# Row skewness on one core: wider loads at the start, part of the row sums on ACT, and the last two blocks closed together

## The chip, the cores and the metric

The kernel runs on one core of one Trainium2 chip. The metric is the device time of one execution in microseconds (us); lower is better. Engines are named as in the profile: PE (TensorE), DVE (VectorE), ACT (ScalarE), POOL (GpSimd), SP (SyncE, which issues the transfers here).

## The reference

The input `x` is 1024 x 8192 in float32 (33.55 MB). For each row the skewness is wanted:

```python
mean = np.mean(x, axis=-1, keepdims=True)
std = np.std(x, axis=-1, keepdims=True)
z = (x - mean) / (std + 1e-8)
return np.mean(z ** 3, axis=-1)
```

Both kernels compute it from three sums of each row: m1 = sum(x)/n, m2 = sum(x^2)/n, m3 = sum(x^3)/n. With var = m2 - m1^2 the result is (m3 - 3 m1 (var + m1^2/3)) * var^-1.5.

## The kernel before, in words

The 1024 rows are 8 blocks of 128 rows, one row a partition. A block's 8192 columns are loaded in units, whose widths stand in `UNITS`, one list a block. A unit is named (block, number), both from 0: (6,2) is the third unit of block 6. The loop at L118 goes over the blocks, the loop at L123 over the units of one. SP issues one load a unit (L125) into one of `X_BUFS` = 8 buffers, so a load waits until the unit eight places earlier has been read by all.

Each unit is cut in equal pieces of at most 2304 columns (`_slices`). For a piece:

- ACT squares it, scaled so that the sum is m2's share, into `sq` (four buffers), and adds up along the row (`accum_out`, L135). A second, short instruction reads the accumulator.
- DVE multiplies `sq` by `x` and adds up along the row (L139): the third sums. This instruction is called a cube below.

PE adds up the columns of a block: it transposes each 128 x 128 piece of `x` against the identity, accumulating all 64 of a block in one PSUM tile `tp` (L145). When the block is through, ACT copies `tp` to `tsb` (L115) and a matmul with a column of 1/8192 gives m1 in one column of `s1ps` (L116).

Each piece's second and third sum has a column of its own in `s2u` and `s3u`; block 7 has its own tiles `s2l` and `s3l`. When block 6 is through, `finish_first_blocks` closes blocks 0 to 6 together: two reduces on DVE (L97), three operations on ACT (L101 to L103), six on POOL (L106 to L111), the power var^-1.5 among them. Block 7 is closed at the end: its m2 by an accumulating copy on ACT (L156), its m3 by a reduce on DVE (L157), m1 squared, variance and the bracket on ACT (L160, L161, L164, L165), the power on POOL (L163), and the numerator on DVE (L166) and the product (L169). Then PE transposes the 128 x 8 results (L172), DVE copies them from PSUM (L174), and SP writes them out (L175).

In the last two units of block 7 the squares go to PSUM (`psq`) and the cubes to a small tile `cubes`, instead of both to the same SBUF buffer.

A scheduler that works from the order of the program sets the order of the instructions on each engine; an instruction whose operands are late can be passed by a later one.

Of the kernel before, what the change touches and what calls it, by code (L numbers as in the profile page):

```python
# [8 lines left out]
FP = mybir.dt.float32  # L9
AF = mybir.ActivationFunctionType  # L10
ALU = mybir.AluOpType
X_AXIS = mybir.AxisListType.X


UNITS = [
    [512, 1024, 2560, 4096],
    [4096, 4096],
    [4096, 4096],
    [4352, 3840],
    [3328, 2816, 2048],  # L20
    [2048, 2048, 2048, 2048],
    [1792, 1792, 1664, 1536, 1408],
    [1152, 1152, 1152, 1152, 1024, 896, 896, 512, 256],
]
SUB_MAX = 2304
X_BUFS = 8
SQ_BUFS = 4
PSUM_SQ = 2


def _slices(w):
    n = -(-w // SUB_MAX)
    step = -(-w // n // 128) * 128
    return [(s, min(s + step, w)) for s in range(0, w, step)]


@with_exitstack
def kernel(
    ctx: ExitStack,
    tc: tile.TileContext,  # L40
    x: bass.AP,
    out: bass.AP,
):
    nc = tc.nc
    P = nc.NUM_PARTITIONS
    R, C = x.shape
    NB = R // P
    L = NB - 1
    inv_n = 1.0 / float(C)
    s_scale = float(C) ** -0.5  # L50
    third = (1.0 / 3.0) ** 0.5
    assert len(UNITS) == NB and all(sum(u) == C for u in UNITS)

    xv = x.rearrange("(b p) c -> b p c", p=P)
    ob = out.rearrange("(b p) -> b p", p=P)


    n_sub = [sum(len(_slices(w)) for w in u) for u in UNITS]
    MAXC = max(n_sub[:L])
    NL = n_sub[L]  # L60

    xpool = ctx.enter_context(tc.tile_pool(name="xp", bufs=X_BUFS))
    sqpool = ctx.enter_context(tc.tile_pool(name="sqp", bufs=SQ_BUFS))
    onep = ctx.enter_context(tc.tile_pool(name="onep", bufs=1))
    psum = ctx.enter_context(tc.tile_pool(name="ps", bufs=2, space=bass.MemoryType.PSUM))
    psq = ctx.enter_context(tc.tile_pool(name="psq", bufs=2, space=bass.MemoryType.PSUM))
    psum1 = ctx.enter_context(tc.tile_pool(name="ps1", bufs=1, space=bass.MemoryType.PSUM))

    onesn = onep.tile([P, 1], FP, tag="onesn")
    nc.vector.memset(onesn, inv_n)  # L70
    tiny = onep.tile([P, 1], FP, tag="tiny")
    nc.scalar.activation(out=tiny, in_=onesn, func=AF.Square)  # L72
    ident = onep.tile([P, P], FP, tag="ident")
    make_identity(nc, ident)
    s2u = onep.tile([P, L * MAXC], FP, tag="s2u")
    s3u = onep.tile([P, L * MAXC], FP, tag="s3u")
    nc.vector.memset(s2u, 0.0)
    nc.vector.memset(s3u, 0.0)
    s2l = onep.tile([P, NL], FP, tag="s2l")
    s3l = onep.tile([P, NL], FP, tag="s3l")  # L80
    cubes = onep.tile([P, 512], FP, tag="cubes")
    junk = onep.tile([P, NL], FP, tag="junk")
    expo = onep.tile([P, L], FP, tag="expo")
    nc.gpsimd.memset(expo, -1.5)
    skew = onep.tile([P, NB], FP, tag="skew")
    s1ps = psum1.tile([P, NB], FP, tag="s1ps")

    Tsb = [onep.tile([P, P], FP, tag=f"tsb{i}", name=f"tsb{i}") for i in range(2)]

    def small(name, n):  # L90
        return onep.tile([P, n], FP, tag=name, name=name)

    def finish_first_blocks():

        m2, m3 = small("m2a", L), small("m3a", L)
        for dst, src in ((m2, s2u), (m3, s3u)):
            nc.vector.tensor_reduce(  # L97
                out=dst, in_=src.rearrange("p (b c) -> p b c", c=MAXC), axis=X_AXIS, op=ALU.add
            )
        m1sq, m1sq3, nm1 = small("m1sqa", L), small("m1sq3a", L), small("nm1a", L)  # L100
        nc.scalar.activation(out=m1sq, in_=s1ps[:, 0:L], func=AF.Square)  # L101
        nc.scalar.activation(out=m1sq3, in_=s1ps[:, 0:L], func=AF.Square, scale=third)
        nc.scalar.activation(out=nm1, in_=s1ps[:, 0:L], func=AF.Copy, scale=-3.0)  # L103
        g = nc.gpsimd
        var, rr = small("vara", L), small("rra", L)
        g.tensor_tensor(out=var, in0=m2, in1=m1sq, op=ALU.subtract)  # L106
        g.tensor_tensor(out=m1sq3, in0=m1sq3, in1=var, op=ALU.add)  # L107
        g.tensor_tensor(out=m1sq3, in0=m1sq3, in1=nm1, op=ALU.mult)  # L108
        g.tensor_tensor(out=m3, in0=m3, in1=m1sq3, op=ALU.add)  # L109
        g.tensor_tensor(out=rr, in0=var, in1=expo, op=ALU.pow)  # L110
        g.tensor_tensor(out=skew[:, 0:L], in0=m3, in1=rr, op=ALU.mult)  # L111

    def close_block(b, tp):
        tsb = Tsb[b % 2]
        nc.scalar.copy(out=tsb, in_=tp)  # L115
        nc.tensor.matmul(out=s1ps[:, b : b + 1], lhsT=tsb, rhs=onesn, start=True, stop=True)  # L116

    for b, widths in enumerate(UNITS):  # L118
        last = b == L
        tp = psum.tile([P, P], FP, tag="tp", name=f"tp_{b}")  # L120
        c0 = 0
        j = 0
        for k, w in enumerate(widths):  # L123
            xt = xpool.tile([P, w], FP, tag="x", name=f"x_{b}_{k}")
            nc.sync.dma_start(out=xt, in_=xv[b, :, c0 : c0 + w])  # L125
            c0 += w
            for s, e in _slices(w):
                i = b * MAXC + j
                a2 = s2l[:, j : j + 1] if last else s2u[:, i : i + 1]
                a3 = s3l[:, j : j + 1] if last else s3u[:, i : i + 1]  # L130
                j += 1
                in_psum = last and k >= len(widths) - PSUM_SQ
                pool = psq if in_psum else sqpool
                sq = pool.tile([P, e - s], FP, tag="sq", name=f"sq_{b}_{k}_{s}")
                nc.scalar.activation(  # L135
                    out=sq, in_=xt[:, s:e], func=AF.Square, scale=s_scale, accum_out=a2
                )
                cube = cubes[:, 0 : e - s] if in_psum else sq
                nc.vector.scalar_tensor_tensor(  # L139
                    out=cube, in0=sq, scalar=1.0, in1=xt[:, s:e],  # L140
                    op0=ALU.mult, op1=ALU.mult, accum_out=a3,
                )
            n = w // P
            for c in range(n):
                nc.tensor.matmul(  # L145
                    out=tp, lhsT=xt[:, c * P : (c + 1) * P], rhs=ident,
                    start=(k == 0 and c == 0), stop=(c0 == C and c == n - 1),
                    is_transpose=True,
                )
        close_block(b, tp)  # L150
        if b == L - 1:
            finish_first_blocks()


    m2, m3 = small("m2l", 1), small("m3l", 1)
    nc.scalar.activation(out=junk, in_=s2l, func=AF.Copy, accum_out=m2)  # L156
    nc.vector.tensor_reduce(out=m3, in_=s3l, axis=X_AXIS, op=ALU.add)  # L157
    m1sq, var, nm1, v3 = small("m1sql", 1), small("varl", 1), small("nm1l", 1), small("v3l", 1)
    p1 = s1ps[:, L:NB]
    nc.scalar.activation(out=m1sq, in_=p1, func=AF.Square)  # L160
    nc.scalar.activation(out=var, in_=m1sq, func=AF.Identity, scale=-1.0, bias=m2)  # L161
    rr = small("rrl", 1)
    nc.gpsimd.tensor_tensor(out=rr, in0=var, in1=expo[:, 0:1], op=ALU.pow)  # L163
    nc.scalar.activation(out=nm1, in_=p1, func=AF.Copy, scale=-3.0)  # L164
    nc.scalar.activation(out=v3, in_=m1sq, func=AF.Identity, scale=1.0 / 3.0, bias=var)  # L165
    nc.vector.tensor_scalar(  # L166
        out=m3, in0=v3, scalar1=nm1, scalar2=m3, op0=ALU.mult, op1=ALU.add
    )
    nc.vector.tensor_tensor(out=skew[:, L:NB], in0=m3, in1=rr, op=ALU.mult)  # L169

    skT_ps = psum1.tile([NB, P], FP, tag="skT")
    nc.tensor.matmul(out=skT_ps, lhsT=skew, rhs=ident, start=True, stop=True, is_transpose=True)  # L172
    skT = small("skT", P)[0:NB, :]
    nc.vector.tensor_copy(out=skT, in_=skT_ps)  # L174
    nc.sync.dma_start(out=ob, in_=skT)  # L175


# [28 lines left out]
```

## Time and profile before

| What | Value |
|---|---|
| median of 4 runs | 92.67 us (92.18 to 92.83) |
| the profiled execution | 92.83 us |
| its span, first to last instruction | 91.0 us |
| busy: DVE, ACT, PE, POOL | 73.9, 69.1, 67.4, 9.4 us |
| loads | 31, 33.56 MB |
| cubes: 41 pieces | 72.7 us |
| squares: 41 pieces | 62.8 us |
| transposes | 512 |

Times in the profile count from the span's start. The profiled execution takes 1.8 us more than its span: what lies ahead of the first and behind the last instruction. A busy share says little here, since four engines and the transfers work on the same unit in turn; what counts is which of them the others wait for, and that changes along the run.

### The profile page before, as it was taken

The numbers are of one execution on the slowest core, as the hardware profiler recorded it, in microseconds if no ns is written. First come the engines' busy times: TensorE is split into PE (matmuls) and PEld (weight loads), VectorE is DVE, ScalarE is ACT, GpSimd is POOL, SyncE is SP. The second block draws the span as 40 slices with busy tenths as digits, with TensorE's granted clock in tenths as the row PEclk, the third lists the DMA queues.
The fourth block names the chain that finished last, engine by engine and source line by source line (L and its number), as shares of the span: only waits on it lengthen the run. The fifth ranks groups of instructions, "written<-read, shape, count | busy, mean of one in ns | idle before, by whom it ended". The sixth has DMA issues, their size and how long they took to land. (4 is left out here: it accounts for less than half of the span.)

```text
span 91.0 us, 1437 instructions
## 1 busy us (share of the span) xinstructions
PE 67.4 (74%) x529; PEld 60.0 (66%) x529; DVE 73.9 (81%) x91; ACT 69.1 (76%) x101; POOL 9.4 (10%) x14
## 2 busy tenths in 40 slices
PE   0390877979495949779789997687789798989610
PEld 0360867779494939578779896577777687867400
DVE  0052290898989798988999999999999999999960
ACT  6350827969595959779799999588798899999820
POOL 3000000000000000000000000000000000799820
PEclk9999999999999999999999999999999999999975
DMA  2999999999999999999999999999999999992000
GB/s 34 370 369 458 439 418 446 425 439 418 432 425 439 427 418 436 426 432 403 436 412 404 436 418 414 421 408 426 413 425 409 407 416 415 404 372 93 0 0 2
DMA packets 4486, 33.64 MB, mean 370 GB/s; under 512 B 504, under 2 KB 640, under 8 KB 2560
## 3 DMA queue, kind: packets, MB, share of 16 engines
q1 hardware_dynamic: 4480, 33.56, 89.0%
q8 instruction: 4, 0.07, 0.3%
q14 instruction: 2, 0.02, 0.0%
HBM read 33.55 MB, written 0.00 MB: 369 GB/s over the span
## 5 line engine op out<-in xcount | busy, mean ns | idle before, releaser
L139 DVE SCALAR_TENSOR_TENSOR sq<-sq,x 128x2048 f32<-128x2048 f32 (+11 forms) x39 | 71.6, 1884 | 13.4 <-ACT sq L135 13.1
L145 PE MATMUL tp<-ident,x 128*128 128x128 f32 x512 | 64.5, 283 | 15.5 <-DMA x<-in_x_dram 15.1
L135 ACT ACTIVATE sq<-x 128x2048 f32<-128x2048 f32 (+12 forms) x41 | 62.8, 1534 | 16.9 <-DMA x<-in_x_dram 15.5
L145 PEld LDWEIGHTS tp<-ident,x 128*128 128x128 f32 x512 | 58.2, 146 | 20.7 <-DMA x<-in_x_dram 16.8
L106 POOL TENSOR_TENSOR vara<-m2a,m1sqa 128x7 f32<-128x7 f32 x1 | 1.3, 1296 | 76.6 <-DVE m3a L97 76.6
L135 ACT ACTIVATION_READ_ACCUMULATOR sq<-x 128x1 f32 x41 | 7.6, 186 | 0.0
L116 PEld LDWEIGHTS s1ps<-onesn,tsb 128*128 128x128 f32 x16 | 2.4, 188 | 5.6 <-ACT tsb L115 5.6
L116 PE MATMUL s1ps<-onesn,tsb 128*128 128x1 f32 x16 | 3.1, 260 | 3.7 <-ACT tsb L115 3.7
L139 DVE DVE_READ_ACCUMULATOR sq<-sq,x 128x1 f32 x39 | 3.2, 81 | 0.0
L110 POOL TENSOR_TENSOR rra<-vara,expo 128x7 f32<-128x7 f32 x1 | 2.6, 2623 | 0.0
L115 ACT COPY tsb<-tp 128x128 f32<-128x128 f32 x8 | 2.0, 249 | 0.0
L172 PE MATMUL skT_ps<-ident,skew 128*8 128x128 f32 x1 | 0.4, 377 | 2.0 <-DVE skew L169 2.0
L72 ACT ACT_TABLE_LOAD x1 | 1.3, 1283 | 0.7 <-PEq L190 0.7
L172 PEld LDWEIGHTS skT_ps<-ident,skew 128*8 128x8 f32 x1 | 0.1, 83 | 2.1 <-DVE skew L169 2.1
L107 POOL TENSOR_TENSOR m1sq3a<-m1sq3a,vara 128x7 f32<-128x7 f32 x1 | 1.2, 1199 | 0.1
L139 DVE SCALAR_TENSOR_TENSOR cubes<-sq,x 128x512 f32<-128x512 f32 (+1 forms) x2 | 1.1, 554 | 0.1
L108 POOL TENSOR_TENSOR m1sq3a<-m1sq3a,nm1a 128x7 f32<-128x7 f32 x1 | 1.1, 1148 | 0.0
L109 POOL TENSOR_TENSOR m3a<-m3a,m1sq3a 128x7 f32<-128x7 f32 x1 | 0.9, 935 | 0.1
L111 POOL TENSOR_TENSOR skew<-m3a,rra 128x7 f32<-128x7 f32 x1 | 0.9, 935 | 0.1
L70 DVE MEMSET onesn<- 128x1 f32 x1 | 0.1, 59 | 0.8 <-PEq L190 0.8
L174 DVE COPY skT<-skT_ps 8x128 f32<-8x128 f32 x1 | 0.3, 279 | 0.5 <-PE skT_ps L172 0.5
L163 POOL TENSOR_TENSOR rrl<-varl,expo 128x1 f32<-128x1 f32 x1 | 0.6, 562 | 0.6 <-ACT varl L161 0.6
(25 smaller groups left out, 4.4 us busy)
## 6 DMA issues: line engine op xcount, KB each, us to landing
x<-in_x_dram SPq DMA_DIRECT2D x5, 2048.0 KB, 18.8
x<-in_x_dram SPq DMA_DIRECT2D x5, 1024.0 KB, 24.5
x<-in_x_dram SPq DMA_DIRECT2D x4, 576.0 KB, 9.8
x<-in_x_dram SPq DMA_DIRECT2D x1, 2176.0 KB, 33.8
x<-in_x_dram SPq DMA_DIRECT2D x1, 1920.0 KB, 36.2
x<-in_x_dram SPq DMA_DIRECT2D x2, 896.0 KB, 15.4
x<-in_x_dram SPq DMA_DIRECT2D x1, 1664.0 KB, 34.0
x<-in_x_dram SPq DMA_DIRECT2D x1, 1408.0 KB, 30.2
```

The source lines that it names most:

```text
L72: nc.scalar.activation(out=tiny, in_=onesn, func=AF.Square)
L106: g.tensor_tensor(out=var, in0=m2, in1=m1sq, op=ALU.subtract)
L107: g.tensor_tensor(out=m1sq3, in0=m1sq3, in1=var, op=ALU.add)
L108: g.tensor_tensor(out=m1sq3, in0=m1sq3, in1=nm1, op=ALU.mult)
L109: g.tensor_tensor(out=m3, in0=m3, in1=m1sq3, op=ALU.add)
L110: g.tensor_tensor(out=rr, in0=var, in1=expo, op=ALU.pow)
L111: g.tensor_tensor(out=skew[:, 0:L], in0=m3, in1=rr, op=ALU.mult)
L115: nc.scalar.copy(out=tsb, in_=tp)
L116: nc.tensor.matmul(out=s1ps[:, b : b + 1], lhsT=tsb, rhs=onesn, start=True, stop=True)
L135: nc.scalar.activation(out=sq, in_=xt[:, s:e], func=AF.Square, scale=s_scale, accum_out=a2)
L139: nc.vector.scalar_tensor_tensor(out=cube, in0=sq, scalar=1.0, in1=xt[:, s:e], op0=ALU.mult, op1=ALU.mult, accum_out=a3,)
L145: nc.tensor.matmul(out=tp, lhsT=xt[:, c * P : (c + 1) * P], rhs=ident, start=(k == 0 and c == 0), stop=(c0 == C and c == n - 1), is_transp ...
```

## The change

What it does:

- The widths. Blocks 0 to 3 are two units of 4096 each; before, block 0 began with 512, 1024 and 2560 and block 3 was 4352 and 3840. From block 4 on the widths shrink to about 1152, and the last unit is 1152 wide (256 before). 31 loads become 27 and 41 pieces become 36.
- In the first unit of blocks 0, 1 and 2, ACT adds up the last 1024 columns (`S1_ACT`) by an accumulating copy, and PE transposes only the other 3072. DVE adds the two parts of m1 for these blocks after block 4.
- `close_first_blocks` closes blocks 0 to 5 after block 5 (before: blocks 0 to 6 after block 6), with a copy of m1 out of PSUM ahead of it.
- Blocks 6 and 7 are each closed by six operations on ACT (`close_on_act`). Block 6's are spread in pairs between the units of block 7. The last of the six writes the term with m1 as one more column of the block's third sums, so that one reduce on DVE gives the numerator; the operation of L166 is gone. One power on POOL and one product on DVE then serve both blocks.
- `s2u` and `s3u` serve all blocks, with K = 8 columns each.
- Only the last unit's square goes to PSUM, and its cube to an `sq` buffer.

The diff, cut to its core:

```diff
 UNITS = [
-    [512, 1024, 2560, 4096],
-    [4096, 4096],
-    [4096, 4096],
-    [4352, 3840],
-    [3328, 2816, 2048],
-    [2048, 2048, 2048, 2048],
-    [1792, 1792, 1664, 1536, 1408],
-    [1152, 1152, 1152, 1152, 1024, 896, 896, 512, 256],
+    [4096, 4096],
+    [4096, 4096],
+    [4096, 4096],
+    [4096, 4096],
+    [3584, 2304, 2304],
+    [2304, 2304, 2048, 1536],
+    [1664, 1792, 1920, 1664, 1152],
+    [1024, 1024, 1152, 1280, 1408, 1152, 1152],
 ]
+S1_ACT = {(0, 0): 1024, (1, 0): 1024, (2, 0): 1024}
...
-PSUM_SQ = 2
+EARLY = 6
...
-    def finish_first_blocks():
+    def close_first_blocks():
...
+        nc.scalar.copy(out=m1a[:, nw:F], in_=s1ps[:, nw:F])
+        nc.scalar.activation(out=m1sq, in_=m1a, func=AF.Square)
...
+    def close_on_act(b):
+        m2, m1sq, nm1, v3 = (small(f"{t}_{b}", 1) for t in ("m2", "m1sq", "nm1", "v3"))
+        p1 = s1ps[:, b : b + 1]
+        var = var2[:, b - F : b - F + 1]
+        act = nc.scalar.activation
+        yield act(out=junk, in_=s2u[:, b * K : b * K + K], func=AF.Copy, accum_out=m2)
+        yield act(out=m1sq, in_=p1, func=AF.Square)
+        yield act(out=var, in_=m1sq, func=AF.Identity, scale=-1.0, bias=m2)
+        yield act(out=nm1, in_=p1, func=AF.Copy, scale=-3.0)
+        yield act(out=v3, in_=m1sq, func=AF.Identity, scale=1.0 / 3.0, bias=var)
+        yield act(
+            out=s3u[:, b * K + K - 1 : b * K + K], in_=v3, func=AF.Identity, scale=nm1
+        )
...
+            w_act = S1_ACT.get((b, k), 0)
+            if w_act:
+                nc.scalar.activation(
+                    out=same[:, 0:w_act], in_=xt[:, w - w_act : w], func=AF.Copy,
+                    scale=inv_n, accum_out=s1a[:, b : b + 1],
+                )
-            n = w // P
+            n = (w - w_act) // P
...
+            if k > 0:
+                next(pending, None)
+                next(pending, None)
...
+        if b == F - 2:
+            nc.vector.tensor_tensor(
+                out=m1a[:, 0:nw], in0=s1ps[:, 0:nw], in1=s1a, op=ALU.add
+            )
+        if b == F - 1:
+            close_first_blocks()
+        if b >= F:
+            pending = close_on_act(b)
+    for _ in pending:
+        pass
...
-    nc.vector.tensor_scalar(
-        out=m3, in0=v3, scalar1=nm1, scalar2=m3, op0=ALU.mult, op1=ALU.add
-    )
-    nc.vector.tensor_tensor(out=skew[:, L:NB], in0=m3, in1=rr, op=ALU.mult)
+    rr = small("rr2", NB - F)
+    nc.gpsimd.tensor_tensor(out=rr, in0=var2, in1=expo[:, 0 : NB - F], op=ALU.pow)
+    num = small("num2", NB - F)
+    nc.vector.tensor_reduce(
+        out=num, in_=s3u[:, F * K :].rearrange("p (b c) -> p b c", c=K), axis=X_AXIS, op=ALU.add
+    )
+    nc.vector.tensor_tensor(out=skew[:, F:NB], in0=num, in1=rr, op=ALU.mult)
```

## The prediction

> **What bounds the kernel now.** I read the page first (slices of the span, queues), then the timelines of PE's weight loads, of DVE and of ACT, because the shares alone mislead: DVE is the busiest engine (73.9 of 91.0 us), yet it doesn't set the pace. The page:
>
> ```profile
> DVE  0052290898989798988999999999999999999960
> DMA  2999999999999999999999999999999999992000
> GB/s 34 370 369 458 439 418 446 425 439 418 432 425 439 427 418 436 426 432 403 436 412 404 436 418 414 421 408 426 413 425 409 407 416 415 404 372 93 0 0 2
> q1 hardware_dynamic: 4480, 33.56, 89.0%
> ```
>
> The transfers never pause from 2.3 to 82 us; one queue brings 33.56 MB. The two slices 2.3 to 6.8 us run at 370 GB/s, the later ones with wide rows at about 430. DVE has holes until 41 us and none over 0.2 us from there to the end of the cubes. SP waits 65.8 us for DVE to free x buffers, but the 2048 KB loads take 18.8 us from issue to landing: the queue is always filled ahead, so this wait costs nothing.
>
> When a load has landed is seen in PE's weight loads, which start some 0.05 us after it (idle time ended by "DMA x"):
>
> ```profile
> 14.27 3.48 PEld L145 LDWEIGHTS tp<-ident,x 128*128 128x128 f32 x32 [1.32 <-DMA x<-in_x_dram]
> 19.17 3.48 PEld L145 LDWEIGHTS tp<-ident,x 128*128 128x128 f32 x32 [0.46 <-DMA x<-in_x_dram]
> ...
> 64.39 1.73 PEld L145 LDWEIGHTS tp<-ident,x 128*128 128x128 f32 x16 [0.75 <-DMA x<-in_x_dram]
> ...
> 70.78 1.41 PEld L145 LDWEIGHTS tp<-ident,x 128*128 128x128 f32 x13 [0.51 <-DMA x<-in_x_dram]
> ...
> 78.69 0.96 PEld L145 LDWEIGHTS tp<-ident,x 128*128 128x128 f32 x9 [0.29 <-DMA x<-in_x_dram]
> 80.12 0.97 PEld L145 LDWEIGHTS tp<-ident,x 128*128 128x128 f32 x9 [0.46 <-DMA x<-in_x_dram]
> ```
>
> A 4096-wide load takes 4.90 us (14.27 to 19.17), an 1152-wide one 1.43 (78.69 to 80.12): (4.90 - 1.43) / 2944 = **1.18 ns a column and 0.07 us a load**. DVE, in its unbroken stretches, needs 2.215 us for a 2048 piece and 1.28 for an 1152 piece: **1.042 ns a column and 0.08 us a piece**. DVE is thus only slightly faster than the loads, and no loss of the loads is made up quickly. The end of the cubes is the largest, over all units U, of: landing of U, + 0.04, + its first square on ACT (0.206 us + 0.837 ns a column, from 1.92 for 2048 and 1.17 for 1152), + 0.12 to DVE, + all DVE work from U on.
>
> Test on unit (6,2) (block 6, third load), landed 70.78: its cube starts at 72.58, only 0.16 after its square ends at 72.42. From there 12800 columns x 1.042 = 13.34, 12 pieces 0.96, the two reduces of L97 0.23: 87.11; measured 87.34, and 0.17 of the difference is the step from 86.13 to 86.91 of a 512 piece whose square is in PSUM (0.61 by the rule). The widths shrink just as the loads need it: nearly every late unit binds. After the cubes:
>
> ```profile
> 87.26 0.08 DVE L139 DVE_READ_ACCUMULATOR cubes<-sq,x 128x1 f32 x1
> 87.38 0.16 DVE L157 TENSOR_REDUCE m3l<-s3l 128x1 f32<-128x9 f32 x1
> 87.66 0.27 DVE L166 TENSOR_SCALAR m3l<-v3l,nm1l,m3l 128x1 f32<-128x1 f32 x1
> 88.03 0.16 DVE L169 TENSOR_TENSOR skew<-m3l,rrl 128x1 f32<-128x1 f32 x1
> ```
>
> and beside them, on ACT, the small chain from the last copy:
>
> ```profile
> 85.59 0.24 ACT L115 COPY tsb<-tp 128x128 f32<-128x128 f32 x1
> ...
> 86.30 0.17 ACT L160 ACTIVATE m1sql<-s1ps 128x1 f32<-128x1 f32 x1 [0.27 <-PE s1ps L116]
> 86.36 0.17 ACT L164 ACTIVATE nm1l<-s1ps 128x1 f32<-128x1 f32 x1
> 86.50 0.29 ACT L161 ACTIVATE varl<-m1sql,m2l 128x1 f32<-128x1 f32 x1
> 86.83 0.29 ACT L165 ACTIVATE v3l<-m1sql,varl 128x1 f32<-128x1 f32 x1
> ```
>
> It ends at 87.12, inside the cubes' cover. The output is issued at 88.97, the span ends 2.0 later.
>
> **What the Trainium skill says.** "VectorE: DVE Perf Modes", Side-by-side, has 2293 ns for 2048 elements in the 1x mode; the trace has 2290, so no shape here can be had cheaper. "ScalarE: Activation LUTs", What ACT_TABLE_LOAD costs, prices an ACTIVATE at 186 ns + 0.833 ns an element and a pointer operand at 93 ns more; the trace has 1058 for 1024 (rule: 1039) and 295 for the small ones with a pointer. Its Step-by-step section says that ACT writes PSUM with less latency than SBUF: a 512 square took 0.63 us into SBUF and 0.58 into PSUM. "DMA: Bandwidth & Descriptors", Bandwidth, names a fixed overhead per packet and a ceiling of 435 GB/s; the fitted 0.07 us a load and the slices of 418 to 446 agree.
>
> **The change, part by part.**
>
> *Loads.* 31 become 27: 2 fewer in block 0, 2 fewer in blocks 6 and 7. At 0.07 each: 0.14 earlier by column 49152, 0.29 at the end. The start is not shown by the trace for wide rows. Full rate in place of 370 GB/s in those two slices is (430 - 370) x 4.55 us = 0.27 MB, 0.65 us at 420: that is the most to be won. Nothing is won if the slow start belongs to the first microseconds whatever the width; and it can be lost: wide rows may suffer longer (rival 2, 0.7 late). I take **0.35 earlier**, the middle of the first two.
>
> *Landings.* (5,3), column 49152, before 64.39: now 64.39 - 0.14 - 0.35 = 63.90. Then by the rule: (6,0) 65.93, (6,1) 68.11, (6,2) 70.45, (6,3) 72.48, (6,4) 73.91, (7,0) 75.19, (7,1) 76.47, (7,2) 77.90, (7,3) 79.48, (7,4) 81.21, (7,5) 82.64, (7,6) 84.07.
>
> *DVE.* 41 pieces become 36; 5 x 0.08 = 0.4 us less, mostly hidden under the loads. Largest sums: (7,4), 1408 wide: 81.21 + 0.04 + 1.38 + 0.12 = 82.75, then 3712 columns 3.87 and 3 pieces 0.24: **86.86**. (6,2): 72.42 + 12928 columns 13.47 + 10 pieces 0.80 = 86.69. (7,6): 85.40 + 1.28 = 86.68. Early: (3,1) lands at 43.28, DVE from 45.36, 36864 columns 38.41, 22 pieces 1.76, small operations 0.4: 85.9. So losing the narrow start loads is free: through the first unit (some 9 us, all 65536 columns) it is 82. With 0.1 for the PSUM piece the cubes end at **86.95** instead of 87.34.
>
> *ACT sums.* Three copies of 1024, 1.06 + 0.19 each. In a pair of units ACT has 4 x 1.92 + 0.25 + 1.25 = 9.2 of 9.8 us: the next square is at most 0.3 late, cover the wait for the loads there (0.97 to 1.00 idle). If it is gone: 0.3 in blocks 0 to 2, which bind by 1 to 3 us less than the late units. PE loses 24 transposes that nobody waits for.
>
> *Close of blocks 0 to 5.* Moved one block earlier, with an added copy on ACT and an add on DVE (about 0.2 each, by the reduce and L101). Behind the copy, squares of block 6 are queued; ACT waits 0.40 for DVE at (6,1) anyway. The add stands behind block 4's cubes, m1 waits for it, no late unit does. POOL's six operations (8 us) shift with them and lie beside cubes that kept their durations before.
>
> *Close of block 6 in block 7.* Six ACT operations, 0.1 to 0.4 each, about 1.2 us, in pairs before units (7,2) to (7,4). ACT there has 0.25 free a unit (1.43 a load, 1.17 a square); behind the third pair waits square (7,4), by at most 0.1. Without that cover 0.4 on (7,4), which binds: that is my upper bound.
>
> *Tail.* The last unit is 1152 wide, not 256. Its square ends at 84.11 + 1.17 = 85.28; PE's 9 transposes at about 85.45, so the copy starts at 85.50 (85.59 before). Copy to square of the mean 0.71, to the variance 0.20, to v3 0.33, to the new column of the third sums 0.33 and 0.29 long: 87.36. The reduce now waits for ACT, from 87.42, not for the cubes (86.95). L166 is gone; the multiply follows the reduce by 0.28: 87.70. The power, two columns wide: 0.56 for one, (2.62 - 0.56) / 6 = 0.34 for each more, so 0.9 from 86.78: 87.68, just hidden; at 0.56 it has slack. From multiply to output issue 0.94: **88.64, against 88.97: 0.33 less.** Removed 0.37 (L166), but ACT's wait of 0.47 takes its place.
>
> The profiled execution took 92.83 with span 91.0, so 90.67 gives 92.50; it stood 0.16 above the median of 92.67, so **92.3**.
>
> **Rivals.** 0.5% is 0.46 us, about what a measurement of this kernel can tell from no change.
>
> 1. *The start wins nothing.* Everything lands 0.35 later and the tail follows one to one: 92.7. For it: the whole gain of the forecast is the start, since fewer loads only pay for the wider end. Against: the fewer loads are certain.
> 2. *Slower: the wide start costs.* If the sixteen engines lose time in proportion to the row at the start, block 0 lands later. The third load of before (2560 wide, 9.38 - 5.06 = 4.32 us, rule 3.09) lost 1.2; for 4096 that is 1.97, so 0.75 more, less 0.29 for fewer loads: 0.4 to 0.5 later than before at every late unit. With the tail of above and 0.1 for the third pair, 93.3. It decides if (0,1) lands after 14.7 (14.27 before).
> 3. *The start wins all, and ACT's chain is shorter* (the scheduler moves the small operations up): 0.65 and 0.3 from the tail, end by cubes: 91.8.
> 4. *The change doesn't do what it says*: block 6's close is scheduled behind block 7's squares and lengthens ACT's last chain by 1.2 us: 93.5. Against: L101 to L103 slipped between squares before.
>
> **How the numbers follow.** Forecast 0.45 (92.0 to 92.6, its half below 92.21 is faster), rival 1 0.2, rival 2 0.16, rival 3 0.15, rival 4 0.04. Faster: half of the forecast 0.23, rival 3's 0.15, 0.02 of rival 1's spread: 0.4. Same: the rest of those two, 0.22 + 0.18: 0.4. Slower: rivals 2 and 4: 0.2. The range runs from rival 3, less 0.3, to rival 2: 91.5 to 93.3.
>
> **What would show it.** (0,1) landing near 13.8; (5,3) near 63.9; (7,4) near 81.2 with its cube within 0.2 of its square; cubes ending near 86.95 and the last reduce 0.4 later, waiting for ACT; power ending before the multiply. Wrong, if the cubes' last stretch has holes, if the first landings are later than before, or if the reduce follows the cubes at once.

## The result, and the profile after

| | before | after |
|---|---|---|
| median of the executions | 92.79 us (92.0 to 94.25, 64 runs) | 92.18 us (91.98 to 92.41, 43 runs) |
| ratio after / before | | 0.9949, 95% interval 0.9935 to 0.9964 |
| profiled execution, its span | 92.83, 91.0 us | 92.04, 90.3 us |
| fastest execution | 92.0 us | 91.98 us |
| last load landed | 84.51 us | 83.64 us |
| cubes end | 87.34 us | 86.66 us |
| output issued | 88.97 us | 87.95 us |

Over all executions the medians differ by 0.61 us (0.7%). The ratio is one of means and leaves out executions more than 1.5% above the fastest of their kernel, 14 of before's 64, so it understates a change that removes long executions. The forecast's ratio (92.3 to 92.67, 0.9960) lies in its interval. The two fastest executions are alike. Before's executions reach 94.25, after's 92.41: the gain is the upper half of before's spread.

The slices of the page after (each a fortieth of the span, 2.26 us; PEclk is the granted clock in tenths), and its queues (packets, MB, share of the engines' time; q8 and q14 fetch instructions):

```profile
DVE  1000598989899298995999999999999999999960
...
PEclk9999999999999996599999999999999999999997
DMA  4899999999999999999999999999999999993000
GB/s 94 349 392 443 457 399 421 465 436 399 443 450 392 421 465 421 392 465 424 407 419 403 433 417 433 412 416 417 422 411 410 411 409 416 413 414 118 0 0 2
...
q1 hardware_dynamic: 3904, 33.56, 89.3%
q8 instruction: 4, 0.07, 0.3%
q14 instruction: 2, 0.02, 0.0%
```

The transfers run without a pause, as before, and late in the kernel at the same 403 to 436 GB/s. The second to fourth slice (349, 392, 443) are no faster than before's (370, 369, 458), only the first moved more (94 against 34). DVE has holes up to slice 19 and none from there to the end of the cubes. PEclk has a hole, at slices 16 and 17.

PE's weight loads show the landings, as before:

```profile
17.85 2.69 PEld L164 LDWEIGHTS tp<-ident,x 128*128 128x128 f32 x24
22.70 3.48 PEld L164 LDWEIGHTS tp<-ident,x 128*128 128x128 f32 x32 [2.17 <-DMA x<-in_x_dram]
...
29.06 2.60 PEld L164 LDWEIGHTS tp<-ident,x 128*128 128x128 f32 x24 [1.92 <-DMA x<-in_x_dram]
...
80.89 1.18 PEld L164 LDWEIGHTS tp<-ident,x 128*128 128x128 f32 x11 [0.66 <-DMA x<-in_x_dram]
...
83.68 0.96 PEld L164 LDWEIGHTS tp<-ident,x 128*128 128x128 f32 x9 [0.41 <-DMA x<-in_x_dram]
```

(1,0) lands before 17.85 and (1,1) at 22.66, some 1.35 us earlier than the same columns before. But (2,0) is there only at 29.02: a unit of 4096 columns took 6.4 us in place of 4.9, and 29.02 is what before had (29.05). Unit (7,4) and the last one are at 80.89 and 83.68.

DVE, from the unit that was to bind to the product:

```profile
79.78 1.36 DVE L151 SCALAR_TENSOR_TENSOR sq<-sq,x 128x1152 f32<-128x1152 f32 x1
...
82.48 1.62 DVE L151 SCALAR_TENSOR_TENSOR sq<-sq,x 128x1408 f32<-128x1408 f32 x1
...
86.58 0.08 DVE L151 DVE_READ_ACCUMULATOR cube<-sqps,x 128x1 f32 x1
86.84 0.17 DVE L188 TENSOR_REDUCE num<-s3u 128x2 f32<-128x16 f32 x1 [0.17 <-ACT s3u L127]
87.11 0.16 DVE L191 TENSOR_TENSOR skew<-num,rr 128x2 f32<-128x2 f32 x1
```

and ACT, with the copies and small operations of the two closes:

```profile
39.39 0.27 ACT L173 COPY tsb<-tp 128x128 f32<-128x128 f32 x1 [1.48 <-PE tp L164]
...
75.65 0.17 ACT L123 ACTIVATE m1sq<-s1ps 128x1 f32<-128x1 f32 x1 [0.27 <-PE s1ps L174]
...
78.51 1.15 ACT L146 ACTIVATE sq<-x 128x1152 f32<-128x1152 f32 x1
...
84.92 0.27 ACT L173 COPY tsb<-tp 128x128 f32<-128x128 f32 x1
...
86.52 0.29 ACT L127 ACTIVATE s3u<-v,nm 128x1 f32<-128x1 f32 x1
```

The reduce waits 0.17 us for ACT's last operation (86.52 + 0.29), not for the cubes. From the cubes' end to the output's issue it is 87.95 - 86.66 = 1.29 us; before it was 88.97 - 87.34 = 1.63. So 0.68 of the profile's gain lies ahead of the cubes' end and 0.34 behind it; of these 1.02 us, 0.7 is left in the span, because from the issue to the span's end it took 2.35 us here and 2.03 before.

**Where the 0.68 comes from.** Every load has sixteen completions in the trace, one for each DMA engine; the last one is the landing. Both ends of that group, in us:

| columns landed | before: first, last, between | after: first, last, between |
|---|---|---|
| 8192 (end of block 0) | 12.51, 14.23, 1.72 | 12.54, 12.87, 0.33 |
| 16384 | 22.30, 24.02, 1.72 | 22.32, 22.66, 0.34 |
| 20480 | 27.19, 29.05, 1.86 | 27.23, 29.02, 1.79 |
| 49152, unit (5,3) | 61.67, 64.34, 2.68 | 61.70, 63.53, 1.83 |
| 65536, the last | 81.88, 84.51, 2.63 | 81.86, 83.64, 1.77 |

The fastest engine arrives at the same time in both kernels, within 0.05 us everywhere. What the change moves is how far the slowest engine is behind; this distance is called the lag below. Before, it falls behind by 1.1 us in the third load (2560 wide) and by another 0.85 at unit (5,1), near 58 us. After, it falls behind once, by 1.45 at (2,0). The last load lands 0.87 earlier, and 0.86 of that is this distance. Before's second step is in ACT's timeline as well, a wait of 1.32 us for (5,1) where the next unit costs 0.42:

```profile
59.52 1.92 ACT L135 ACTIVATE sq<-x 128x2048 f32<-128x2048 f32 x1 [1.32 <-DMA x<-in_x_dram]
61.95 1.92 ACT L135 ACTIVATE sq<-x 128x2048 f32<-128x2048 f32 x1 [0.42 <-DMA x<-in_x_dram]
```

### The profile page after: what moved, and what is told of

It reads as the page before. It is cut to its first block, busy times and chain, and to the rows that moved or that the text cites. A ratio compares the mean times of both kernels' runs of the same rounds, so it can differ in the third digit from the quotient of the medians.

```text
span 90.3 us, 1371 instructions
## 1 busy us (share of the span) xinstructions
PE 65.2 (72%) x505; PEld 59.5 (66%) x505; DVE 73.0 (81%) x81; ACT 72.1 (80%) x106; POOL 11.3 (13%) x14
## 4 chain that ended last, share of the span: by engine, by line
DMA 57%; DVE 21%; PE 7%; ACT 5%; issue 4%; SPq 2%; DVEq 0%
DMA x<-in_x_dram 57%; DVE sq L151 20%; PE tp L164 6%; SPq L139 2%; ACT sq L146 2%; ACT sqps L146 1%; PE s1ps L174 0%; ACT s3u L127 0%; ACT v L126 0%; ACT tsb L173 0%; PE skT_ps L193 0%; DVE skT L195 0%; ACT var L124 0%; DVE num L188 0%; DVE skew L191 0%
## 5 line engine op out<-in xcount | busy, mean ns | idle before, releaser
L151 DVE SCALAR_TENSOR_TENSOR sq<-sq,x 128x2048 f32<-128x2048 f32 (+9 forms) x35 | 70.6, 2070 | 13.5 <-ACT sq L146 13.5
L164 PE MATMUL tp<-ident,x 128*128 128x128 f32 x488 | 62.7, 288 | 17.3 <-DMA x<-in_x_dram 17.2
L146 ACT ACTIVATE sq<-x 128x2048 f32<-128x2048 f32 (+9 forms) x35 | 60.6, 1734 | 10.7 <-DMA x<-in_x_dram 10.1
L109 POOL TENSOR_TENSOR vara<-m2a,m1sqa 128x6 f32<-128x6 f32 x1 | 1.8, 1824 | 67.3 <-DVE m3a L98 67.3
L113 POOL TENSOR_TENSOR rra<-vara,expo 128x6 f32<-128x6 f32 x1 | 3.3, 3258 | 0.0
L158 ACT ACTIVATE same<-x 128x1024 f32<-128x1024 f32 x3 | 3.1, 1040 | 0.0
L110 POOL TENSOR_TENSOR m1sq3a<-m1sq3a,vara 128x6 f32<-128x6 f32 x1 | 1.9, 1867 | 0.1
L151 DVE SCALAR_TENSOR_TENSOR cube<-sqps,x 128x1152 f32<-128x1152 f32 x1 | 1.4, 1353 | 0.0
L112 POOL TENSOR_TENSOR m3a<-m3a,m1sq3a 128x6 f32<-128x6 f32 x1 | 1.2, 1201 | 0.1
L146 ACT ACTIVATE sqps<-x 128x1152 f32<-128x1152 f32 x1 | 1.1, 1137 | 0.1
L123 ACT ACTIVATE m1sq<-s1ps 128x1 f32<-128x1 f32 x2 | 0.3, 171 | 0.5 <-PE s1ps L174 0.5
## 6 DMA issues: line engine op xcount, KB each, us to landing
x<-in_x_dram SPq DMA_DIRECT2D x1, 960.0 KB, 13.1
```

What stands on the lines that cost most here:

```text
L146: nc.scalar.activation(out=sq, in_=xt[:, s:e], func=AF.Square, scale=s_scale, accum_out=s2u[:, j : j + 1],)
L151: nc.vector.scalar_tensor_tensor(out=cube, in0=sq, scalar=1.0, in1=xt[:, s:e], op0=ALU.mult, op1=ALU.mult, accum_out=s3u[:, j : j + 1],)
L158: nc.scalar.activation(out=same[:, 0:w_act], in_=xt[:, w - w_act : w], func=AF.Copy, scale=inv_n, accum_out=s1a[:, b : b + 1],)
L164: nc.tensor.matmul(out=tp, lhsT=xt[:, c * P : (c + 1) * P], rhs=ident, start=(k == 0 and c == 0), stop=(c0 == C and c == n - 1), is_transp ...
```

## The experiments

Theory A, of the start: the gain is the wide first load, that of the close and the late widths is small. Against it stood that the late widths, the shorter tail, the sums on ACT or the joint close make it. The expectations call theories by letters; B is the tail and the closing, C the fewer loads, D the load on PE. The runs were timed on four chips, each beside runs of before on the same chip. Chips differ a little, so a ratio belongs to its chip.

| run | median, range, runs | ratio to before, 95% interval |
|---|---|---|
| chip 12, before | 92.98, 92.17 to 93.64, 46 | |
| s1_wide_start | 92.24, 91.98 to 92.37, 11 | 0.9919, 0.989 to 0.9949 |
| s2_narrow_start | 92.75, 91.97 to 94.08, 22 | 0.9973, 0.9943 to 1.0003 |
| s3_widths_only | 92.38, 92.26 to 92.52, 18 | 0.9939, 0.992 to 0.9957 |
| s4_no_act_sums | 92.15, 92.09 to 92.25, 8 | 0.9929, 0.9891 to 0.9966 |
| chip 5, before | 93.07, 92.12 to 94.89, 59 | |
| s5_wide_then_narrow | 92.25, 92.14 to 92.38, 22 | 0.9942, 0.9922 to 0.9962 |
| s6_two_2048 | 92.09, 91.95 to 92.35, 12 | 0.9919, 0.9892 to 0.9946 |
| s7_dve_term | 92.45, 92.26 to 92.67, 22 | 0.9947, 0.9929 to 0.9964 |
| s8_close_seven | 92.14, 91.99 to 92.40, 16 | 0.9916, 0.9892 to 0.994 |
| chip 2, before | 93.15, 92.69 to 94.03, 11 | |
| s9_1024_first | 92.07, 91.89 to 92.78, 6 | 0.9881, 0.9829 to 0.9934 |
| s10_short_chain | 91.87, 91.69 to 92.01, 6 | 0.9846, 0.9804 to 0.9889 |
| s11_best | 92.22, 92.05 to 92.55, 6 | 0.9889, 0.9844 to 0.9933 |
| chip 9, before | 93.35, 92.72 to 94.70, 11 | |
| s12_close_later | 91.77, 91.69 to 91.89, 6 | 0.9825, 0.9788 to 0.9863 |

### The start alone, put in and taken out

s1_wide_start is before with one line changed:

```diff
-    [512, 1024, 2560, 4096],
+    [4096, 4096],
```

> The kernel before, with block 0 loaded as 4096 and 4096; nothing else is changed. Theory A (the start): the narrow first loads cost the late loads of the kernel before an amount that varies from execution to execution; so this alone gives nearly the whole gain: 92.2 to 92.4, ratio 0.994 to 0.997, (0,1) landing near 12.9, and a spread of its executions like that of the changed kernel (under 0.5 us) instead of 92.0 to 94.25. Theory B (the tail and the closing): 92.8 and the old spread. Theory C (fewer loads late): 92.65, 2 loads at 0.07 us, and the old spread.

s2_narrow_start is after with the opposite edit; the sum on ACT of block 0 goes to its last unit:

```diff
-    [4096, 4096],
+    [512, 1024, 2560, 4096],
...
-S1_ACT = {(0, 0): 1024, (1, 0): 1024, (2, 0): 1024}
+S1_ACT = {(0, 3): 1024, (1, 0): 1024, (2, 0): 1024}
```

> The changed kernel, with block 0 loaded as 512, 1024, 2560, 4096 again and ACT's part of block 0 taken from the last unit. Theory A: the gain is gone and the executions spread again: 92.6 to 92.9, ratio 0.998 to 1.001, single executions above 93. Theory B: as the changed kernel, 92.2, spread under 0.5 us. Theory C: 92.3.

One line in before gave 92.24, all of the gain, and a range of 0.39 us where before's runs on that chip span 1.47. The opposite edit in after took the gain back: the interval of its ratio includes 1, and its runs span 2.11 us again. ACT's timeline of s1_wide_start, first squares of units:

```profile
8.32 1.91 ACT L135 ACTIVATE sq<-x 128x2048 f32<-128x2048 f32 x1 [6.09 <-DMA x<-in_x_dram]
...
13.15 1.92 ACT L135 ACTIVATE sq<-x 128x2048 f32<-128x2048 f32 x1 [0.93 <-DMA x<-in_x_dram]
...
23.00 1.92 ACT L135 ACTIVATE sq<-x 128x2048 f32<-128x2048 f32 x1 [1.00 <-DMA x<-in_x_dram]
...
29.11 1.91 ACT L135 ACTIVATE sq<-x 128x2048 f32<-128x2048 f32 x1 [2.05 <-DMA x<-in_x_dram]
```

PE's weight loads of s2_narrow_start, the first four landings and the last three:

```profile
3.72 0.72 PEld L164 LDWEIGHTS tp<-ident,x 128*128 128x128 f32 x4 [3.72 <-issue]
5.16 1.57 PEld L164 LDWEIGHTS tp<-ident,x 128*128 128x128 f32 x8 [0.73 <-DMA x<-in_x_dram]
9.59 4.13 PEld L164 LDWEIGHTS tp<-ident,x 128*128 128x128 f32 x20 [2.86 <-DMA x<-in_x_dram]
14.49 1.64 PEld L164 LDWEIGHTS tp<-ident,x 128*128 128x128 f32 x11 [0.77 <-DMA x<-in_x_dram]
...
81.95 1.18 PEld L164 LDWEIGHTS tp<-ident,x 128*128 128x128 f32 x11 [0.65 <-DMA x<-in_x_dram]
83.34 0.96 PEld L164 LDWEIGHTS tp<-ident,x 128*128 128x128 f32 x9 [0.21 <-DMA x<-in_x_dram]
84.73 0.97 PEld L164 LDWEIGHTS tp<-ident,x 128*128 128x128 f32 x9 [0.43 <-DMA x<-in_x_dram]
```

s1_wide_start has after's pattern of landings, up to 0.3 us later: 8.3, 13.1, 23.0, then 6.1 us to 29.1. s2_narrow_start repeats before's: 9.59 for the first 4096 columns (before 9.38) and 1.05 us later than after at the end (84.73 against 83.68), although its other widths are after's. Its completions lie 1.71 apart after the third load and 2.63 at the end. The start decided, and not the late part of the change.

### How wide, and how much of it

s5_wide_then_narrow: before, with block 0 as `[4096, 512, 1024, 2560]`. Narrow loads come, but not first.

> The kernel before with block 0 loaded as 4096, 512, 1024, 2560: the same widths, the wide one first. Theory A1: in the first microseconds each DMA engine stalls once on the first rows that it handles of a load (0.3 to 1 us); with wide rows this falls once and alike on all engines, with narrow loads it falls on three loads, unevenly, and the engine that was hit most stays behind. Then only what comes first matters: 92.3 to 92.45 (two more loads than in s1, 0.07 each), executions within 0.5 us. Rival A2: narrow rows stall unevenly wherever they stand in block 0: 92.7 to 93.0, spread of over 1 us.

s6_two_2048: before, with block 0 as `[2048, 2048, 4096]`.

> The kernel before with block 0 loaded as 2048, 2048, 4096. Theory A1: a row of 8 KB takes about 0.31 us, 8 rows a load and engine 2.5 us, so the first load covers most of the first microseconds in which engines stall (up to some 4 us in the profiles with narrow loads): most of the gain, 92.3 to 92.5, spread between the two. Rival A2 (it is the narrow rows of 2 and 4 KB as such): as s1 plus one load, 92.25 to 92.35, tight. Were the number of loads the cause: 92.6.

s9_1024_first: before, with block 0 as `[1024, 3072, 4096]`.

> The kernel before with block 0 loaded as 1024, 3072, 4096. Its first load (8 rows of 4 KB an engine, 1.3 us) ends for most engines while first rows still stall, so by theory A1 the second load's first rows stall again and engines drift apart, if less than with three narrow loads: 92.3 to 92.6, spread 0.5 to 1 us. Rival A3: only the 512 load with its 2 KB rows, or a row of three narrow loads, does harm: 92.1 to 92.2, tight, as with 2048 first.

All three keep the gain: 92.25, 92.09, 92.07. s5 has the 31 loads of before and the median of s1 with its 29 (92.25, 92.24), so the number of loads costs nothing that can be seen, and it isn't narrow loads as such that lose time but narrow loads at the very start. A first load of 2048 is enough; with 1024 first, the completions in the profile lie 0.36 us apart after 4096 columns, as with wide ones, but one of the six runs took 92.78, so that width may be at the border. Six runs can't tell.

For the first 10 us the packets' records add a description, not a cause. Measured against the median row of the same width, and counting rows that lose 0.06 us or more, packets lose about as much time in both ways, summed over the engines (10.4 us before, 8.7 after, 10.3 in s1 and s2, 6.5 in s6). With a wide first load most of the loss falls on the engines' first rows, up to 1.0 us each. With narrow ones it falls on rows of three loads, and some engines lose up to 0.9 us on a single row of the third.

### The rest of the widths, and the sums on ACT

s3_widths_only: before's code with all widths of after (one square in PSUM instead of two, `cubes` 1152 wide).

> The kernel before with all widths of the changed kernel; no sums on ACT, blocks 0 to 6 closed together, block 7 closed with the multiply-add of L166; only the last unit's square in PSUM. Theory A and C: nearly as the changed kernel: the operation of L166 costs 0.2 to 0.3 at the end, the squares of block 7 run without block 6's small operations: 92.2 to 92.45, tight. Theory B: 92.8.

92.38 with all of the widths, 92.24 with the first block's alone: from block 3 on, the new widths cost 0.14 if anything. The fewer loads do not pay for the wider end.

s4_no_act_sums: after with `S1_ACT = {}`, so PE transposes everything and the add on DVE is gone.

> The changed kernel without the sums on ACT: PE transposes all columns, the add on DVE and the three copies are gone. Theory A: no difference, 92.1 to 92.3, since PE is not waited for late. Rival D (PE): in the changed kernel's profile PE has gaps of 2.2 us at 27 to 34 us, its granted clock falls to 0.5 and 0.6 at 34 to 38.6 us, the copy to tsb of block 2 waits 1.48 us and the squares of (3,0) start 0.7 late; without the sums PE's gaps are 0.9 us shorter; if that avoids the low clock, DVE's unbroken stretch starts up to 0.6 earlier at (3,0), with at most 0.1 to 0.2 left at the end, because (6,2) and (7,2) bind then: 92.0 to 92.1. If PE needs the relief in the cold start, 92.4.

92.15 against 92.18 for after: the sums on ACT are worth nothing that can be seen. They were also under suspicion for the hole in PEclk. The windows of s4_no_act_sums (stretch, its length, busy time and instructions of PE, PEld, DVE, ACT and POOL, then clock, DMA share, GB/s):

```profile
24.00:29.00 5.00, 3.00 (x26) 2.67 (x24) 4.62 (x5) 3.00 (x5) 0.00 (x0) 1.00 1.03 439
29.00:34.00 5.00, 4.84 (x29) 4.84 (x30) 3.26 (x5) 3.90 (x4) 0.00 (x0) 0.66 0.99 423
34.00:39.00 5.00, 4.45 (x40) 4.13 (x38) 4.62 (x5) 4.17 (x5) 0.00 (x0) 1.00 0.99 423
```

The clock falls to 0.66 here too, one unit earlier, with no sum on ACT, so these sums aren't what makes it fall. A long wait of PE alone doesn't either: s2_narrow_start, where PE waits 2.11 us for (2,1), has a 9 in every slice up to the last. The last section has what goes with the fall.

### The close

s7_dve_term: after, with block 7's m1 term added behind the reduce by DVE, as before had it at L166:

```diff
-        yield act(
-            out=s3u[:, b * K + K - 1 : b * K + K], in_=v3, func=AF.Identity, scale=nm1
-        )
+        if b == L:
+            term.extend((v3, nm1))
+        else:
+            yield act(
+                out=s3u[:, b * K + K - 1 : b * K + K], in_=v3, func=AF.Identity, scale=nm1
+            )
...
+    nc.vector.tensor_scalar(
+        out=num[:, 1:2], in0=term[0], scalar1=term[1], scalar2=num[:, 1:2],
+        op0=ALU.mult, op1=ALU.add,
+    )
```

> The changed kernel, but block 7's term with m1 is no column of the third sums: DVE adds it after the reduce with a multiply-add, as L166 did. By the step of the prediction: the reduce no longer waits for ACT's last small operation (0.17 in the changed kernel's profile), but an operation of 0.27 with 0.37 to its follower comes in: 0.2 to 0.25 slower than the changed kernel, 92.4. Rival: the wait takes all that the operation cost: 92.2.

Its DVE timeline:

```profile
86.61 0.17 DVE L192 TENSOR_REDUCE num<-s3u 128x2 f32<-128x16 f32 x1
86.89 0.27 DVE L195 TENSOR_SCALAR num<-v,nm,num 128x1 f32<-128x1 f32 x1
87.27 0.16 DVE L199 TENSOR_TENSOR skew<-num,rr 128x2 f32<-128x2 f32 x1
```

The reduce no longer waits, 0.03 behind the cubes (86.58), but the product comes 0.69 behind the cubes' end; in after, 0.45 (86.66 to 87.11). The medians, from two chips, are 92.45 against 92.18: the column is worth about 0.27.

s8_close_seven: after with `EARLY = 7`: blocks 0 to 6 closed together, block 7 alone.

> The changed kernel with EARLY = 7: blocks 0 to 6 closed together after block 6, block 7 alone by six operations on ACT; block 6's small operations are gone from between the squares of block 7. If they hold up (7,1) and (7,2) by about 1 us on ACT, as the profile shows, but DVE's backlog hides it, the cubes end at most 0.1 earlier and the time is 92.1 to 92.2. Rival: POOL's six operations, which took 8.3 us in the kernel before and 10.0 in the changed one, now start near 78 and end at 86.3 to 88: at 88 the last transpose waits for POOL, 0.7 later: 92.9.

92.14, no difference to 92.18 that can be seen. POOL's six operations end at 85.6 there and are still under the cubes. Closing 6 and 7 together is worth nothing by itself.

### Towards a faster kernel

s10_short_chain puts together what cost nothing and shortens ACT's last chain by writing the term as m1 (2 m1^2 - 3 m2):

```diff
-    [4096, 4096],
+    [2048, 2048, 4096],
...
-S1_ACT = {(0, 0): 1024, (1, 0): 1024, (2, 0): 1024}
+S1_ACT = {}
...
-EARLY = 6
+EARLY = 7
...
+        yield act(out=junk, in_=cols, func=AF.Copy, scale=-3.0, accum_out=m2n)
+        yield act(out=q, in_=p1, func=AF.Square, scale=2.0 ** 0.5)
+        yield act(out=m1, in_=p1, func=AF.Copy)
+        yield act(out=var, in_=q, func=AF.Identity, scale=-0.5, bias=m2)
+        yield act(out=v, in_=q, func=AF.Identity, bias=m2n)
```

> The changed kernel with block 0 as 2048, 2048, 4096, no sums on ACT, blocks 0 to 6 closed together (EARLY = 7), and block 7's small chain on ACT one step shorter: the term with m1 is written as m1 (2 m1^2 - 3 m2), with -3 m2 summed beforehand, so that it doesn't wait for the variance. ACT's last operation ends 0.2 to 0.3 earlier than in the changed kernel, the reduce then waits for the cubes alone (0.17 less): 92.0 to 92.1. Rival: the power on POOL (0.56 after the variance) or the cubes end as late as ACT did: 92.15.

DVE of s10_short_chain:

```profile
86.68 0.16 DVE L184 TENSOR_REDUCE num<-s3u 128x1 f32<-128x8 f32 x1
86.94 0.16 DVE L187 TENSOR_TENSOR skew<-num,rr 128x1 f32<-128x1 f32 x1
```

The wait of 0.17 for ACT is gone, and the product comes 0.17 earlier than in after. The medians differ by 0.31, but on two chips; what each of the four edits gives isn't shown.

s11_best adds widths that the prediction's sum (landing, square, all DVE work behind it) gave as best, with block 6 ending in 1280 and block 7 as `[1536, 1408, 1280, 1280, 1024, 896, 768]`.

> As s10, with widths chosen by the sum over units of the prediction (landing, first square, all DVE work from there on), so that no unit binds much ahead of the others: blocks 3 to 7 as 4224, 3968; 3328, 2560, 2304; 2048, 2176, 2048, 1920; 1920, 1792, 1664, 1536, 1280; 1536, 1408, 1280, 1280, 1024, 896, 768. The sum gives cubes that end 0.25 earlier and a last unit of 768 that leaves ACT 0.25 earlier: 91.8 to 91.95. Rival: the squares wait for free sq buffers or for the small operations, and nothing is won: 92.05.

It missed: 92.22, 0.35 more than s10. ACT and then DVE of s11_best:

```profile
76.05 0.16 ACT L101 COPY m1a<-s1ps 128x7 f32<-128x7 f32 x1 [0.47 <-PE s1ps L174]
```

```profile
78.14 1.76 DVE L151 SCALAR_TENSOR_TENSOR sq<-sq,x 128x1536 f32<-128x1536 f32 x1 [0.68 <-ACT sq L146]
```

The sum had left out what s8 had hidden: four operations of the close stand on ACT ahead of the square of (7,0), the first of them waiting 0.47 for the matmul that gives m1. In after and s10, DVE had a backlog over that wait; here the widths had used it up, and DVE stood 0.68. Late landings have a part in this profile: it shows the slowest of the six executions, whose units from (5,3) to (7,3) landed 0.4 to 0.5 later than with the same widths in the profile of s12 below.

s12_close_later issues the close one unit later and reads m1 from PSUM without the copy:

```diff
+            if b == F and k == 0:
+                close_first_blocks()
...
-        nc.scalar.copy(out=m1a[:, nw:F], in_=s1ps[:, nw:F])
-        nc.scalar.activation(out=m1sq, in_=m1a, func=AF.Square)
+        m1 = s1ps[:, 0:F]
+        nc.scalar.activation(out=m1sq, in_=m1, func=AF.Square)
```

> As s11, but the closing of blocks 0 to 6 is issued after the first unit of block 7, and reads m1 from PSUM without the copy. In s11 its four small operations stood ahead of square (7,0) on ACT, the first of them waited 0.47 for the matmul, and DVE idled 0.68 before cube (7,0); nothing after it made that up. If this wait is why s11 was 0.35 slower than s10, the cubes end about 0.65 earlier than in s11 and ACT's last operation binds: 91.7 to 91.85. Rival: POOL's six operations, 5.5 to 8.3 us from about 78.7, end after 86.9 and the last transpose waits for them: 92.0 or more. Second rival: the late loads of s11 land later than in s10 (83.9 against 83.5), and that is the cause: 92.1 to 92.2 again.

DVE of s12_close_later:

```profile
77.39 1.80 DVE L150 SCALAR_TENSOR_TENSOR sq<-sq,x 128x1536 f32<-128x1536 f32 x1 [0.32 <-ACT sq L145]
...
86.70 0.16 DVE L180 TENSOR_REDUCE num<-s3u 128x1 f32<-128x8 f32 x1
86.97 0.16 DVE L183 TENSOR_TENSOR skew<-num,rr 128x1 f32<-128x1 f32 x1
```

91.77 (91.69 to 91.89), ratio 0.9825 with an interval of 0.9788 to 0.9863: the fastest kernel of the study. On ACT the later issue moved nothing: the three operations that are left still stand ahead of that square. What shortened the wait, by the trace, is the dropped copy: from the end of the wait for the matmul to the square it is 0.19 us (75.58 to 75.77), in s11 0.50 (76.05 to 76.55). DVE still waits 0.32. The cube of (7,0) starts 0.75 earlier than in s11's profile; 0.36 of this is the shorter wait, and by the other 0.39 DVE was ahead already, with the earlier landings. It beats s11, and both kernels of the change; that it beats s10 (91.87, another chip) is not shown.

## Why the prediction was right or wrong

The time, 92.3 against 92.18, was right, in part by luck. The forecast gain was 0.37 us, against a median of 4 runs of before (92.67); measured it is 0.61, against one of 64 (92.79). In the profiles the output's issue came 1.02 earlier where 0.33 was said. The largest term, the start with the fewer loads, was too small (0.49 by column 49152 where 0.81 came) and wrong in mechanism; the tail's was too small as well.

- **The start and the loads.** The forecast took 0.35 from a better rate at the start and 0.14, later 0.29, from fewer loads: 0.49 by column 49152, and (5,3) at 63.90. Measured, by the completions, it came at 63.53, 0.81 earlier than before. Neither term is in the trace. On the fastest engine (5,3) came at 61.70 against 61.67 and the last load at 81.86 against 81.88, so neither rate nor load count gave anything there; s5 says the same of the count, so the 0.07 us a load isn't a cost that a removed load gives back. The two early slices stayed as slow (349 and 392 GB/s in after), the case in which the prediction said that nothing is won. The step that failed is to treat sixteen engines as one rate: of the 1.2 us that the third load lost, 1.1 was the lag of the slowest engine, which the narrow start leaves at 1.7 us. The average over the engines couldn't show it, the spread of the completions could.
- **Rival 2, a wide start that loses more.** Wrong. It read the third load's loss as growing with the row and decided at (0,1) landing after 14.7. It landed at 12.87. The loss isn't in proportion to the row: 4096 wide lost less than 2560 wide had in third place.
- **Rivals 1, 3 and 4.** Rival 1, that the start wins nothing, holds for the rate and not for the time. Rival 3 had the sizes nearer than the forecast (0.65 from the start and 0.3 from the tail, where 0.81 and 0.34 came), for the same reason of a better rate. Rival 4 is out: block 6's close ran between block 7's squares and ended at 78.6.
- **Not foreseen: the late unit (2,0).** By it the first 1.36 us of the gain (14.23 to 12.87) were gone at 29 us. Had nothing else happened, the late landings would have been before's. What brought the gain back is a second step of the lag, of 0.85 us at (5,1) before and 0.79 at the same place in s2, so in both profiles with a narrow start. The twelve profiles with a first load of 1024 or more have no step over 0.5 us after 30 us.
- **DVE and the sum over the units.** With the measured landing of (7,4), 80.89 by the weight loads, the sum gives 80.89 + 0.04 + 1.38 + 0.12 + 4.11 + 0.1 = 86.64; measured 86.66. The cost rule held to 0.02, and the forecast's 86.95 is off only by the landing (81.21).
- **The sums on ACT at nothing.** Right: s4.
- **Close of block 6.** The bound was 0.1 late on (7,4), or 0.4 with the cover gone. Measured: L123 waited 0.27 with the square of (7,0) behind it, and the square of (7,2) began at 78.51, 0.98 after its landing at 77.53. That is ten times the 0.1. It cost almost nothing at the end, since DVE was busy without a break from 41.59 and waited only 0.12 for that square. The step that failed is where the delay would fall: not on (7,4), whose square came 0.05 ahead of DVE, but on (7,0) to (7,2), behind the wait for the matmul. The cover it named, DVE's backlog, was there.
- **POOL.** Six operations took 10.1 us (68.56 to 78.65) where 8 was said, hidden. The power over two columns took 0.70, inside 0.56 to 0.9.
- **The tail.** The copy to `tsb` came 1.24 after the last landing where 1.43 was said, so the reduce waited 0.17 for ACT, not 0.47. The step "removed 0.37 (L166), but ACT's wait of 0.47 takes its place" is the second mis-sized term: s7 puts L166 back, and that costs 0.27. The output's issue came at 87.95, 0.69 ahead of the forecast's 88.64: 0.29 by the cubes' end, 0.30 by the smaller wait, 0.10 from product to issue. The time was nearer than that (the profiled execution 92.04 against 92.50, the median 92.18 against 92.3), since the output took 0.3 longer from issue to the span's end, and one profile stands a little off its median both times.
- **Late widths.** Forecast as a gain of 0.15 (two more loads saved) against a wider end; measured 0.14 slower than the start alone (s3 against s1), with intervals of the ratio that overlap.

Three limits lie within 0.2 us of one another in after's profile: DVE's backlog from 41.59 on, the square of (7,2) delayed by the close (DVE waits 0.12 for it), and the landing of (7,4), whose square is there 0.05 before DVE is. That would explain why s4 and s8, which each change one of the first two, move nothing.

**What the packets show of the lag.** On one engine a row of a load begins within about 0.02 us of the end of the one before, so the rows can be put to engines by their times alone. In eleven of the fourteen profiles this gives each engine's course (from the fourth load on in before and s2, to 81.8 us in s6). After the first 10 us an engine falls behind there only where a packet that fetches instructions stands between its rows: by 1.5 to 1.7 us for one of 16 KB, by 0.7 to 1.1 for one of 8 KB. In after, such a fetch at 26.44 takes 1.10 us and the next row 0.47 more than its usual 0.61; this engine goes from 0.28 us behind the fastest to 1.82. Each of these profiles has six fetches, on six different engines, so what counts is how far behind the engine already was. After a wide start that was 0.3 to 0.7 us at most, and the first 16 KB fetch (22 to 27 us) makes one unit between 24 and 29 us land 1.1 to 1.7 late. All twelve of these profiles have this late unit behind such a fetch; nine of them are among the eleven. Before and in s2, the 8 KB fetch at 57.9 and 57.7 fell on the very engine that the third load had left last, and took it from 1.8 to 2.8 and from 1.65 to 2.6 us. The 16 KB fetch at 23.4 and 28.4 fell on others there, and so added only 0.14 and 0.06 to the lag.

**Left open.** Why engines lose different amounts in the first microseconds, and what decides on which engine a fetch falls, isn't settled; no run moved or removed a fetch. That the spread of before's executions (92.0 to 94.25) is the lag of a different size each time is an inference from two narrow profiles against the tight ranges of all wide ones; no short and long execution of one kernel were both profiled. It would fit: by an estimate from the figures above, a 16 KB fetch on the last engine gives some 3.3 us (1.8 + 1.55), and none on it about what a wide start gives.

## What to carry to other kernels

This kernel, which streams at full rate, ends with the slowest of its DMA engines: look at the first and the last of a load's completions before pricing a load in bytes a second, and at the range of the executions as well as the median. Starting small to get the engines going earlier can leave them uneven. That need not cost anything by itself (at 29 us both kernels had the same lag), but here it did once a later delay fell on an engine that was already behind. A first load of 2048 columns or more won 0.7 to 1.0 us, and the later start of DVE cost nothing, because it had slack up to 41 us. And when widths are tuned until every unit binds, each small operation in front of a square has to be in the sum, with its wait.

## What was not expected of the hardware

- The distance between the first and the last of the sixteen engines, once there, stays: 1.72 to 1.89 us from 9 to 56 us before, 1.76 to 1.85 from 29 us to the end after. In no profile did it shrink by more than 0.21 us.
- At the end it was 2.63 in both profiles with a narrow start and 1.57 to 2.25 in the twelve others, with the fastest engine's last completion at 81.66 to 82.17 in all.
- Fetching instructions is not free for the data: a 16 KB fetch held one of the sixteen engines up by about 1.55 us, and a load has landed only when its last engine is through.
- PE's granted clock halved for 3.41 us in the middle of nine of the fourteen profiles (0.66 as the mean of a stretch of 5 us), and 32 transposes took some 5.1 us in place of 3.5. ACT's copy waited 1.48 us for it. The Trainium skill, "TensorE: Matmul & The Clock Gate", Part 1, gives half rate after an idle window of about 3.4 us and calls the window free-running. Here all changes of the clock lie whole steps of 3.41 us apart. It halved after every step in which PE's matmuls left 1.73 us or more idle (23 times, the ends of the kernels included), and after none with 1.72 or less: half a step was enough. A wait that falls across two steps did nothing: in s6 PE waited 2.89 us for (1,1) at full clock, while in s1 two waits of 0.44 and 1.58 us in one step, before (2,0), halved it.
